# Two-block network on one core: S5 preparation in fine pieces with loads from GpSimd's queue, S5 recurrence steps behind every second weight split, first S5 outputs behind the third projection

## Chip, cores and metric

One core of a Trainium2 chip (trn2). The metric is the device time of one execution in microseconds, as the median of several runs. The kernel is one launch; weights are read from HBM once.

## The reference, cut to what matters

A sequence of 256 rows with 1024 features goes through two layers of a first block and then two layers of a second one. All is float32. A layer of the first block is

```python
h = h + 0.5 * rmsnorm(swiglu(rmsnorm(h)))       # FFN1, hidden width 2816
h = h + rmsnorm(mixer(rmsnorm(h)))
h = h + 0.5 * rmsnorm(swiglu(rmsnorm(h)))       # FFN2
```

The mixer projects its input to z, xbc, dt, u5 and two gates, and joins two branches: an SSD branch (convolution, chunked state-space sum, gated norm; four groups) and an S5 branch:

```python
step = exp(log_step); lam_bar = exp(lam * step)             # complex, 64 groups x 64 states
b_bar = ((lam_bar - 1.0) / lam)[..., None] * b
bu = einsum("blgc,gnc->blgn", u5, b_bar)
states = associative_scan(combine, (lam_bar, bu))            # s_t = lam_bar * s_(t-1) + bu_t
y = real(einsum("blgn,gcn->blgc", states, c)) + d_skip * u5
val, gate = split(gelu(y) @ w_glu)                           # then val * sigmoid(gate)
```

Everything of S5 that depends on weights alone (powers of lam_bar, products of b and c with them) is what is called S5 preparation below.

## The kernel before

**Weights and units.** Every weight matrix is streamed in units of 128x1024 floats (`unit`, L1563 and on). SyncE's queue loads a unit into a raw buffer (L1571), ScalarE casts it to a high part (`hi`, L1576), VectorE subtracts to get the low part (`lo`, L1577: this is called the split), and TensorE makes three matmuls per tile (high by high, high by low, low by high). The pair of parts comes from a ring of buffers; some entries of the ring are S5's buffers while S5 doesn't need them, and are dropped in time. During FFN1 of either layer it comes down to five pairs. `stream_b` (L1600 and on) streams column chunks: a unit is then 24 matmuls of 256 columns. `stream_k` streams a down projection: a unit is 12 matmuls of 512 columns; its last six units run the second row tile late (`TAIL`).

**FFN1 and S5 preparation.** A feed-forward stage has six chunks of hidden columns (c0 with both row tiles led by `lead_b`, c1 to c5 through `stream_b`, gate and up; 36 units in c1 to c5) and 22 units of the down projection (d0 to d21). After a chunk or unit it calls `aside`. FFN1 uses this to step a generator, `prep`, at the points of the table `PREP`: in layer 0 at c0 to c4, d0, d3, d6, d9 and d12 (constants of the mixer and S5, then four quarters q of S5, and the power tables in two halves), in layer 1 at c1, c2, c4, d1 and d6 (only the quarters). Each step is a large lump. The small matmuls of a quarter (`s5_products`, 64 of 64x64) come later, by `product()`, at points of their own. In FFN2 of layer 0 the power tables of layer 1 are made at d2 and d8.

A quarter consists of: `s5_wb` (L324 and on), which loads two tables of 512 KB from SyncE's queue (`s5B` L331 and `s5L` L333), makes four tensor operations on GpSimd (L341 to L344) and stores the result `Wd` from GpSimd's queue; `s5_cb`, two loads of 128 KB (`s5c` L351 from SyncE, `s5b` L352 from GpSimd); `s5_ct`, six VectorE products of 512 columns (L372 to L377) and two ScalarE copies; `s5_products`, the matmuls, a ScalarE copy out of PSUM, six VectorE operations (L404 to L415) and two stores `Td` from GpSimd's queue. Its big buffers are the four of the list `pp`, one each for `s5B`, `s5L`, `s5CF` and `s5bq`, so the next quarter reuses them.

**Power tables.** `s5_powers_prep(l, h)` doubles powers six times, to 63, for 16 of a layer's 32 groups of states at a time, with 36 VectorE operations (L301 to L303) per half, and stores three tables `Ed`.

**Mixer.** `mixer_body` makes u5, stores and reloads it, and puts S5's input through `s5_z`. Then the string `ORDER` says what is traced in turn: p is an SSD projection (8 units, convolution on VectorE, L569), d the time steps (1 unit), g a gate (4 units), o a quarter of the S5 outputs, c the core of an SSD group. The recurrence `s5_rec` is a generator of 14 VectorE steps for each half of the states (12 products at L545 and two scans at L549); the 28 steps are chained as `side`, and `stream_b` calls `beside()` once per unit, right behind the unit's split, which takes the next step. The outputs o0 and o1 need the first 14 steps, o2 and o3 all of them. The S5 loads of `s5_y`, the tables of the second half and SSD's broadcast rows come from GpSimd's queue.

**What sets the order.** The kernel is traced in the order of the code. A scheduler then orders each engine's instructions by readiness with the order of the code as priority; `issue_after(x)` adds the condition that the instructions traced inside it come behind x on x's own engine. With `last_lo` this holds VectorE's instructions behind the latest split, with `last_mm` TensorE's behind the latest matmul, with `last_pow` GpSimd's behind the latest norm's power. Numbered buffers (`q0` to `q16`) are shared through the lists of each stage: `X`, `W`, `A`, `E` and so on; a new use waits for the end of the old one. `X` (u5, gates, S5 loads and outputs) and `W` (two temporaries of the recurrence) share 2 and 3.

Of the kernel before, what the change touches and what calls it, by code (L numbers as in the profile page):

```python
# [30 lines left out]
ORDER = "p0 d p1 g0 g1 o0 o1 p2 c0 g2 c1 p3 o2 o3 g3 c2 c3".split()  # L31
# [4 lines left out]
    "X": [2, 3, 0, 1], "U": [4, 5], "A": [12, 13, 6, 7, 8, 9, 10, 11, 12, 13, 6, 7, 8, 9, 6, 7], "M": [15, 16],  # L36
# [42 lines left out]
class Mixer:  # L79
# [58 lines left out]
    def mix_prep(self, I):  # L138
# [109 lines left out]

        self.FL = ct.tile([P, 3, 4, NL], F32, name="FL")
        fi = t("fli")  # L250
        for d in range(4):
# [7 lines left out]
            v.tensor_scalar_mul(self.FL[:, 2, d, :], self.FL[:, 0, d, :], -1.0)  # L259

# [20 lines left out]
    def s5_powers_prep(self, l, h):  # L281


        g = self.nc.gpsimd
        tt = self.nc.vector.tensor_tensor
        Ed = self.Ed[l, h] = self.dram.tile([3, P, 1024], F32, tag="Ed", name=self.nm("Ed"), bufs=4)
        if True:
            E = [self.slot("B", "E").rearrange("p (a i) -> p a i", i=64) for _ in range(3)]
            Et = self.slot("B", "Et").rearrange("p (k a i) -> p k a i", k=2, i=32)
            x, y = Et[:, 0], Et[:, 1]  # L290
# [13 lines left out]
            for r in range(3):  # L304
                g.dma_start(Ed[r], E[r].rearrange("p a i -> p (a i)"))
# [1683 lines left out]
```

## Time and profile before

| what | us |
|---|---|
| median of 3 runs (lowest to highest) | 2936.93 (2934.03 to 2939.28) |
| the profiled execution | 2936.55 |
| its span, first to last instruction | 2934.5 |
| TensorE busy | 2814.3 (96%) |
| VectorE busy | 2181.6 (74%) |
| ScalarE busy | 1674.2 (57%) |
| GpSimd busy | 206.0 (7%) |

PE is TensorE, PEld its weight loads, DVE VectorE, ACT ScalarE, POOL GpSimd, SP SyncE. Lines (L1577) are those of the kernel before, and a helper's line stands for all its callers. A wait is the idle time of an engine before an instruction, put down to what ended it. Matmuls overlap in the pipeline, so the duration of one says little; how many start in a stretch says more. The granted clock of TensorE is a share of full speed.

### The profile page before, as it was taken

How to read it: one execution, taken by the hardware profiler on the slowest of the kernel's cores; microseconds unless marked ns; L12 is line 12 of the kernel's file. 1: busy time of each engine (PE TensorE's matmuls, PEld its weight loads, DVE VectorE, ACT ScalarE, POOL GpSimd, SP SyncE). 2: the span in 40 equal slices, each digit the busy share in tenths (PEclk: the TensorE clock that was granted, in tenths of full speed). 3: DMA queues.
4: the chain of work that ended last, by engine and by line, in shares of the span. 5: the costliest groups of instructions: out<-in, count | busy, mean ns of one | idle time of the engine just before them, and what ended most of it. 6: DMA issues, size and time to landing. Idle time of an engine off the chain costs nothing. (4 is left out here: it accounts for less than half of the span.)

```text
span 2934.5 us, 49144 instructions
## 1 busy us (share of the span) xinstructions
PE 2814.3 (96%) x19040; PEld 2508.2 (85%) x19040; DVE 2181.6 (74%) x3043; ACT 1674.2 (57%) x2389; POOL 206.0 (7%) x257
## 2 busy tenths in 40 slices
PE   8979999999999999999999999999999999999997
PEld 7968888999979888888999898987678888888886
DVE  5886877765667758777755566555589999999997
ACT  5434456545445444475554445445377777777776
POOL 2140001000004100010000000000000000000000
PEclk9999999999999999999999999999899999999998
DMA  7677565576567775656855646654589999999993
GB/s 238 199 250 242 160 204 164 197 227 188 184 223 249 241 221 174 194 155 196 264 171 180 215 154 192 186 192 132 184 279 356 343 361 361 343 359 356 354 344 145
DMA packets 350928, 687.88 MB, mean 234 GB/s; under 512 B 32672, under 2 KB 121952, under 8 KB 350688
## 3 DMA queue, kind: packets, MB, share of 16 engines
q1 hardware_dynamic: 336592, 637.42, 65.9%
q0 software_dynamic: 13952, 46.74, 4.8%
q8 instruction: 151, 2.47, 0.3%
q14 instruction: 89, 0.73, 0.1%
q10 hardware_dynamic: 144, 0.52, 0.0%
HBM read 658.05 MB, written 26.54 MB: 233 GB/s over the span
## 5 line engine op out<-in xcount | busy, mean ns | idle before, releaser
L1577 DVE TENSOR_TENSOR lo<-raw,hi 128x1024 fp32r<-128x1024 f32 x646 | 788.6, 1230 | 296.8 <-ACT hi L1576 285.1
L1576 ACT CAST hi<-raw 128x1024 fp32r<-128x1024 f32 x646 | 674.9, 1048 | 455.6 <-PE accmo L1587 84.6
L1586 PE MATMUL accmo<-lo,xg 128*128 128x512 f32 (+1 forms) x768 | 289.7, 378 | 2.3 <-DVE lo L1577 2.3
L1587 PE MATMUL accmo<-hi,xg 128*128 128x512 f32 (+1 forms) x768 | 285.2, 372 | 0.0
L1585 PE MATMUL accmo<-hi,xg 128*128 128x512 f32 (+1 forms) x768 | 274.0, 373 | 1.4 <-ACT hi L1576 1.4
L1577 DVE TENSOR_TENSOR big<-raw,big 128x1024 fp32r<-128x1024 f32 x147 | 184.9, 1259 | 110.2 <-ACT big L1576 109.3
L1576 ACT CAST big<-raw 128x1024 fp32r<-128x1024 f32 x147 | 153.7, 1049 | 168.0 <-issue 31.1
L1577 DVE TENSOR_TENSOR part<-raw,part 128x1024 fp32r<-128x1024 f32 x111 | 135.3, 1223 | 85.5 <-ACT part L1576 83.1
L1576 ACT CAST part<-raw 128x1024 fp32r<-128x1024 f32 x111 | 116.1, 1050 | 114.2 <-DMA raw<-in_ffn_w_gate_dram 17.4
L1586 PEld LDWEIGHTS accmo<-lo,xg 128*128 128x128 f32 x768 | 144.6, 188 | 32.3 <-DVE lo L1577 5.6
L1585 PEld LDWEIGHTS accmo<-hi,xg 128*128 128x128 f32 x768 | 144.6, 188 | 28.1 <-ACT hi L1576 2.6
L1587 PEld LDWEIGHTS accmo<-hi,xg 128*128 128x128 f32 x768 | 144.8, 189 | 22.5
L1586 PE MATMUL accmo<-lo,th 128*128 128x512 f32 x352 | 138.0, 392 | 0.0
L1587 PE MATMUL accmo<-hi,th 128*128 128x512 f32 x352 | 137.7, 391 | 0.0
L1577 DVE TENSOR_TENSOR lo<-big,hi 128x1024 fp32r<-128x1024 f32 x88 | 106.6, 1223 | 10.7 <-ACT hi L1576 7.6
L1585 PE MATMUL accmo<-hi,th 128*128 128x512 f32 x352 | 109.2, 391 | 0.0
L1576 ACT CAST hi<-big 128x1024 fp32r<-128x1024 f32 x88 | 92.7, 1054 | 27.0 <-PE accmo L1587 26.7
L1592 PE MATMUL accfa<-xh,lo 128*128 128x256 f32 x352 | 99.8, 284 | 0.0
L1591 PE MATMUL accfa<-xh,hi 128*128 128x256 f32 x352 | 99.7, 283 | 0.0
L1593 PE MATMUL accfa<-xl,hi 128*128 128x256 f32 x352 | 99.7, 284 | 0.0
L1577 DVE TENSOR_TENSOR lo<-more,hi 128x1024 fp32r<-128x1024 f32 x68 | 82.3, 1223 | 7.0 <-ACT hi L1576 5.0
L1576 ACT CAST hi<-more 128x1024 fp32r<-128x1024 f32 x68 | 71.4, 1053 | 19.3 <-PE accmo L1587 17.8
(993 smaller groups left out, 8603.3 us busy)
## 6 DMA issues: line engine op xcount, KB each, us to landing
raw<-in_w_gu_moe_dram SPq DMA_DIRECT2D x190, 512.0 KB, 5.3
raw<-in_w_in_dram SPq DMA_DIRECT2D x128, 512.0 KB, 4.4
raw<-in_w_down_moe_dram SPq DMA_DIRECT2D x94, 512.0 KB, 5.6
raw<-in_ffn_w_gate_dram SPq DMA_DIRECT2D x88, 512.0 KB, 4.1
raw<-in_ffn_w_up_dram SPq DMA_DIRECT2D x88, 512.0 KB, 4.3
raw<-in_ffn_w_down_dram SPq DMA_DIRECT2D x88, 512.0 KB, 4.2
big<-in_w_gu_moe_dram SPq DMA_DIRECT2D x60, 512.0 KB, 5.7
more<-in_w_gu_moe_dram SPq DMA_DIRECT2D x46, 512.0 KB, 5.7
```

What stands on the lines that cost most here:

```text
L1576: nc.scalar.copy(hi, raw)
L1577: self.last_lo = nc.vector.tensor_tensor(lo, raw, hi.bitcast(F32), op=ALU.subtract).ins
L1585: mm(ps, lh, rh, start=first, stop=False)
L1586: mm(ps, lh, rl, start=False, stop=False)
L1587: self.last_mm = mm(ps, ll, rh, start=False, stop=last).ins
L1591: mm(ps, lh, rh, start=first, stop=False)
L1592: mm(ps, ll, rh, start=False, stop=False)
L1593: self.last_mm = mm(ps, lh, rl, start=False, stop=last).ins
```

## The change

- `ORDER`: p2 now comes before o0 and o1. The list `X` is longer, so that 2 and 3 stay free for the recurrence until the second gate g2.
- `beside()` takes a step only every `pace`-th unit. `pace` is 2 inside the projections p0, p1 and p3, and 1 otherwise.
- The table `PREP`, `product()` and the list of late products go. `prep` becomes `side` at the end of chunk 0 (layer 0) or 1 (layer 1) of FFN1, with one step behind every unit's split; `stream_k` calls `beside()` too, for the units ahead of its tail. What is left behind FFN1 is run off there.
- The generators yield much more often: 17 pieces of the constants, 11 of the powers, five for each quarter (two coefficient products in each of the first three, nothing in the fourth, the small matmuls and what follows them in the fifth).
- `s5B`, `s5L` and `s5c` are loaded from GpSimd's queue instead of SyncE's.
- `s5_powers_prep(l)` makes powers to 31 for all 32 groups at once (30 VectorE operations), in six doublings less one, and ScalarE copies them out to tables of 64, the lower half conjugated and in reverse. Layer 0's come before the quarters, layer 1's from the end of chunk 4 of FFN2.
- In the products, the first masked copy moves from VectorE to ScalarE.

The diff, cut to its core (the added bare `yield` lines of `mix_prep` are left out):

```diff
-ORDER = "p0 d p1 g0 g1 o0 o1 p2 c0 g2 c1 p3 o2 o3 g3 c2 c3".split()
+ORDER = "p0 d p1 g0 g1 p2 o0 o1 c0 g2 c1 p3 o2 o3 g3 c2 c3".split()
...
-    "X": [2, 3, 0, 1], "U": ...
+    "X": [2, 3, 0, 1, 0, 1, 0, 1, 0] + [2, 3, 1, 0] * 5, "U": ...
...
-PREP = (
-    ("c0 c1 c2 c3 c4 d0 d3 d6 d9 d12".split(), "d0 d4 d10 d15".split()),
-    ("c1 c2 c4 d1 d6".split(), "c4 d1 d6 d11".split()),
-)
...
-    def s5_powers_prep(self, l, h):
+    def s5_powers_prep(self, l):
+        E = [self.slot("B", "E").rearrange("p (a i) -> p a i", i=32) for _ in range(2)]
+        Et = self.slot("B", "Et").rearrange("p (k a i) -> p k a i", k=2, i=16)
+        x, y = Et[:, 0], Et[:, 1]
+        for r in range(2):
+            g.memset(E[r][:, :, 0], 1.0 - r)
+            cp(E[r][:, :, 1], self.s4dir[:, r, l * 32 : l * 32 + 32])
+        for n in (1, 2, 4, 8, 16):
+            k = min(n, 31 - n)
+            b = [e[:, :, n : n + 1].to_broadcast([P, 32, k]) for e in E]
+            for r, op in ((0, ALU.subtract), (1, ALU.add)):
+                tt(x[:, :, :k], E[0][:, :, 1 : k + 1], b[r], op=ALU.mult)
+                if n > 8:
+                    yield
+                tt(y[:, :, :k], E[1][:, :, 1 : k + 1], b[1 - r], op=ALU.mult)
+                tt(E[r][:, :, n + 1 : n + 1 + k], x[:, :, :k], y[:, :, :k], op=op)
+                if n > 4:
+                    yield
+            if n < 8:
+                yield
+        for h in range(2):
...
+            for r in range(2):
+                g.memset(F[r][:, :, 0], 0.0)
+                cp(F[r][:, :, 32:], E[r][:, hs])
+                self.nc.scalar.activation(F[r][:, :, 1:32], E[r][:, hs, :0:-1], AF.Copy, scale=1.0 - 2.0 * r)
+            g.memset(F[2][:, :, 0], 0.0)
+            cp(F[2][:, :, 1:], self.s4len[:, ls].unsqueeze(2).to_broadcast([P, 16, 63]))
             for r in range(3):
-                g.dma_start(Ed[r], E[r].rearrange("p a i -> p (a i)"))
+                g.dma_start(Ed[r], F[r].rearrange("p a i -> p (a i)"))
+            yield
...
         cb = [self.s5_cb(I, l, 0)]
-        yield
+        if l == 0:
+            yield from self.s5_powers_prep(0)
         for q in range(4):
             self.s5_wb(I, l, q)
             if q < 3:
                 cb.append(self.s5_cb(I, l, q + 1))
-            self.late.append(self.s5_ct(l, q, *cb.pop(0)))
-            yield
-            if l == 0 and q in (1, 2):
-                self.s5_powers_prep(0, q - 1)
-                yield
+            yield from self.s5_ct(l, q, *cb.pop(0))
...
-        nc.sync.dma_start(B, I["s5_bT"][l, q])
+        nc.gpsimd.dma_start(B, I["s5_bT"][l, q])
...
-        nc.sync.dma_start(Lb, ld.unsqueeze(1).to_broadcast([8, 16, 1024]))
+        nc.gpsimd.dma_start(Lb, ld.unsqueeze(1).to_broadcast([8, 16, 1024]))
...
-        self.nc.sync.dma_start(cc, I["s5_cT"][l, q])
+        self.nc.gpsimd.dma_start(cc, I["s5_cT"][l, q])
...
         tt(u, ce(1), fl(1), op=ALU.mult)
+        yield
         tt(Cv[:, :, 0], Cv[:, :, 0], u, op=ALU.add)
         tt(Cv[:, :, 1], ce(0), fl(1), op=ALU.mult)
+        yield
...
-        return lambda: self.s5_products(q, p0, bq, CF, s)
+        yield
+        yield
+        with self.tc.issue_after(self.last_mm):
+            self.s5_products(q, p0, bq, CF, s)
+        yield
...
-        nc.vector.tensor_scalar_mul(T, K, self.jm[:, 0:1])
+        nc.scalar.activation(T, K, AF.Copy, scale=self.jm[:, 0:1])
...
     def beside(self):
+        self.beat += 1
+        if self.beat % self.pace:
+            return
         with self.tc.issue_after(self.last_lo):
             next(self.side, None)
...
         def proj(g):
+            self.pace = 1 if g == 2 else 2
             pr[g] = self.ssd_proj(W, l, g, xh, xl)
+            self.pace = 1
...
             if i < nk - kk * tail:
+                self.beside()
+            if i < nk - kk * tail:
                 go(0, u, k0)
                 go(1, u, k0)
-                if aside:
-                    aside(f"d{i}")
...
             if w == f"c{l}":
                 self.ring_drop((6, 7), (8, 9))
-            if w in at[1]:
-                self.product()
-            if w in at[0]:
-                with self.tc.issue_after(self.last_lo), self.tc.issue_after(self.last_pow.ins):
-                    next(steps, None)
+                self.side = self.prep(I, l)
+                if l == 0:
+                    with self.tc.issue_after(self.last_lo), self.tc.issue_after(self.last_pow.ins):
+                        next(self.side)
-        return self.swiglu(*xT, *w, aside)()
+        banks = self.swiglu(*xT, *w, aside)()
+        with self.tc.issue_after(self.last_lo):
+            for _ in self.side:
+                pass
+        return banks
...
-            if l == 0 and w in ("d2", "d8"):
-                with self.tc.issue_after(self.last_lo):
-                    self.s5_powers_prep(1, "d2 d8".split().index(w))
+            if l == 0 and w == "c4":
+                self.side = self.s5_powers_prep(1)
```

## Rows read from the trace of the kernel before

**Rows 1.** The page: busy time by engine; the costliest group of ScalarE.
```profile
PE 2814.3 (96%) x19040; PEld 2508.2 (85%) x19040; DVE 2181.6 (74%) x3043; ACT 1674.2 (57%) x2389; POOL 206.0 (7%) x257
...
L1576 ACT CAST hi<-raw 128x1024 fp32r<-128x1024 f32 x646 | 674.9, 1048 | 455.6 <-PE accmo L1587 84.6
```
**Rows 2.** Stretches: us, then busy us (instructions) of PE, PEld, DVE, ACT, POOL, clock.
```profile
50.00:100.00 50.00, 50.00 (x419) 50.00 (x418) 35.08 (x90) 25.02 (x36) 0.00 (x0) 1.00 0.62 181
311.50:400.70 89.20, 77.72 (x582) 75.90 (x577) 81.85 (x110) 37.16 (x61) 3.25 (x6) 0.90 0.53 166
400.70:432.50 31.80, 31.32 (x402) 30.34 (x402) 19.60 (x31) 17.20 (x30) 2.67 (x5) 1.00 0.67 215
...
856.30:1051.00 194.70, 193.12 (x1478) 177.43 (x1478) 133.28 (x153) 90.46 (x120) 50.57 (x38) 0.99 0.74 234
```
**Rows 3.** TensorE's instructions by tile: ns min/median/max, first to last start; layers 0, 1.
```profile
L1585 PE MATMUL accfa<-hi,hh x52: 387/389/628, 150.3 to 238.5; 128*128 128x512 f32 x52
...
L1585 PE MATMUL accfa<-big,hh x36: 387/389/628, 152.4 to 239.9; 128*128 128x512 f32 x36
...
L1585 PE MATMUL accfa<-big,hh x40: 389/389/504, 988.2 to 1055.7; 128*128 128x512 f32 x40
...
L1585 PE MATMUL accmx<-part,xh x16: 389/389/792, 247.7 to 268.3; 128*128 128x512 f32 x16
...
L1585 PE MATMUL accmx<-part,xh x16: 387/389/498, 1059.8 to 1079.3; 128*128 128x512 f32 x16
```
**Rows 4.** Timeline near 195 us: start, us, instructions merged.
```profile
194.81 0.81 PE L396 MATMUL zfa<-s5CF,s5bq 64*64 64x64 f32 x20
```
**Rows 5.** TensorE's waits from 100 to 262 us: total, times, longest.
```profile
PE zfa L396 <- DVE s5CF L374: 7.5, 1, 7.5
...
PE accfa L1591 <- DVE ht L1827: 2.8, 1, 2.8
```
**Rows 6.** SyncE's waits from 100 to 262 us: total, times, longest.
```profile
SPq L333 <- POOL s5B L342: 19.9, 3, 9.2
...
SPq L331 <- DMA Wd<-s5B: 18.5, 3, 11.1
```
**Rows 7.** GpSimd's operations on s5t from 100 to 262 us: ns min/median/max.
```profile
L341 POOL TENSOR_TENSOR s5t<-s5B,s5L x4: 2413/2862/4560, 127.0 to 207.3; 128x1024 f32<-128x1024 f32 x4
L343 POOL TENSOR_TENSOR s5B<-s5B,s5t x4: 1264/1468/2150, 132.3 to 216.0; 128x512 f32<-128x512 f32 x4
```
**Rows 8.** VectorE's S5 operations by tile from 100 to 262 us: ns min/median/max.
```profile
L375 DVE TENSOR_TENSOR s5CF<-s5c,FL x4: 684/685/2905, 127.0 to 205.4; 128x512 f32<-128x512 f32 x4
...
L301 DVE TENSOR_TENSOR Et<-E,E x12: 199/352/2422, 157.6 to 233.0; 128x16 f32<-128x16 f32 x2, 128x32 f32<-128x32 f32 x2, 128x64 f32<-128x64 f32 x2, 128x128 f32<-128x128 f32 x2
L302 DVE TENSOR_TENSOR Et<-E,E x12: 190/248/669, 157.7 to 233.5; 128x16 f32<-128x16 f32 x2, 128x32 f32<-128x32 f32 x2, 128x64 f32<-128x64 f32 x2, 128x128 f32<-128x128 f32 x2
...
L414 DVE SCALAR_TENSOR_TENSOR s5u<-s5u,jm x12: 343/480/2498, 167.1 to 241.4; 128x384 f32<-128x384 f32 x4, 128x256 f32<-128x256 f32 x4, 128x128 f32<-128x128 f32 x4
```
**Rows 9.** DMA issues from 100 to 262 us: KB each, median us to landing.
```profile
Wd<-s5B POOLq DMA_DIRECT2D x4, 512.0 KB, 7.5
...
s5c<-in_s_cT_dram SPq DMA_DIRECT2D x4, 128.0 KB, 6.4
...
s5b<-in_s_bS_dram POOLq DMA_DIRECT2D x2, 128.0 KB, 6.8
```
**Rows 10.** GpSimd's issue of the s5b load by tile: ns min/median/max.
```profile
L352 POOL DMA_DIRECT2D s5b<-in_s_bS_dram x6: 541/551/601, 174.1 to 999.7; - x6
```
**Rows 11.** The recurrence of layer 0 on VectorE by tile: ns min/median/max.
```profile
L545 DVE TENSOR_TENSOR S<-S x4: 1205/1212/1219, 317.7 to 397.2; 128x1024 f32<-128x1024 f32 x4
...
L549 DVE TENSOR_TENSOR_SCAN S<-s5E,S x4: 2272/2283/2285, 322.2 to 384.8; 128x1024 f32<-128x1024 f32 x4
```
**Rows 12.** VectorE's groups from 311.5 to 400.7 us: busy us, mean ns, idle before.
```profile
L1577 DVE TENSOR_TENSOR part<-raw,part 128x1024 fp32r<-128x1024 f32 x6 | 7.3, 1214 | 0.5 <-ACT part L1576 0.5
...
L569 DVE SCALAR_TENSOR_TENSOR cv<-accpa,cw,cv 128x255 f32<-128x255 f32 (+2 forms) x12 | 5.1, 471 | 0.0
```

More of the change, by code (lines that the diff above doesn't have):

```diff
@@ L264, in mix_prep @@
         cmul(*u2, (cs, sn), (cs, sn))
+        yield
         cmul(self.s4dir[:, 0], self.s4dir[:, 1], u2, u2)
@@ L279, in mix_prep @@
         dma(self.lsd.rearrange("k a x -> a k x"), lt.rearrange("p g j r n -> p (g j) (r n)"))
-    def s5_powers_prep(self, l, h):
+    def s5_powers_prep(self, l):
         g = self.nc.gpsimd
+        cp = self.nc.scalar.copy
         tt = self.nc.vector.tensor_tensor
[L286 to L290, printed above, removed]
-            ls = slice(l * 32 + h * 16, l * 32 + h * 16 + 16)
-            g.memset(E[2][:, :, 0], 0.0)
-            self.nc.scalar.copy(E[2][:, :, 1:], self.s4len[:, ls].unsqueeze(2).to_broadcast([P, 16, 63]))
-            for r in range(2):
-                g.memset(E[r][:, :, 0], 1.0 - r)
-                self.nc.scalar.copy(E[r][:, :, 1], self.s4dir[:, r, ls])
-            for n in (1, 2, 4, 8, 16, 32):
-                k = min(n, 63 - n)
-                b = [e[:, :, n : n + 1].to_broadcast([P, 16, k]) for e in E[:2]]
-                for r, op in ((0, ALU.subtract), (1, ALU.add)):
-                    tt(x[:, :, :k], E[0][:, :, 1 : k + 1], b[r], op=ALU.mult)
-                    tt(y[:, :, :k], E[1][:, :, 1 : k + 1], b[1 - r], op=ALU.mult)
-                    tt(E[r][:, :, n + 1 : n + 1 + k], x[:, :, :k], y[:, :, :k], op=op)
@@ new lines, in s5_powers_prep @@
+        E = [self.slot("B", "E").rearrange("p (a i) -> p a i", i=32) for _ in range(2)]
[10 more added lines that the diff above has]
+                if n > 8:
+                    yield
+                tt(y[:, :, :k], E[1][:, :, 1 : k + 1], b[1 - r], op=ALU.mult)
+                tt(E[r][:, :, n + 1 : n + 1 + k], x[:, :, :k], y[:, :, :k], op=op)
+                if n > 4:
+                    yield
+            if n < 8:
+                yield
@@ new lines, in s5_powers_prep @@
+        for h in range(2):
+            Ed = self.Ed[l, h] = self.dram.tile([3, P, 1024], F32, tag="Ed", name=self.nm("Ed"), bufs=4)
+            hs = slice(h * 16, h * 16 + 16)
+            F = [self.slot("B", "Eh").rearrange("p (a i) -> p a i", i=64) for _ in range(3)]
+            for r in range(2):
[3 more added lines that the diff above has]
+            g.memset(F[2][:, :, 0], 0.0)
+            ls = slice(l * 32 + h * 16, l * 32 + h * 16 + 16)
+            cp(F[2][:, :, 1:], self.s4len[:, ls].unsqueeze(2).to_broadcast([P, 16, 63]))
@@ L373, in s5_ct @@
         tt(u, ce(1), fl(1), op=ALU.mult)
+        yield
         tt(Cv[:, :, 0], Cv[:, :, 0], u, op=ALU.add)
         tt(Cv[:, :, 1], ce(0), fl(1), op=ALU.mult)
+        yield
         tt(u, ce(1), fl(2), op=ALU.mult)
@@ L383, in s5_ct @@
             )
-        return lambda: self.s5_products(q, p0, bq, CF, s)
+        yield
+        yield
+        with self.tc.issue_after(self.last_mm):
+            self.s5_products(q, p0, bq, CF, s)
+        yield
     def s5_products(self, q, p0, bq, CF, s):
@@ L1431, in __init__ @@
         self.side = iter(())
+        self.beat, self.pace = 0, 1
         self.Ed = {}
@@ L1842, in ffn1 @@
         w = [I[f"ffn1_w_{k}"][l] for k in ("gate", "up", "down")]
-        steps = self.prep(I, l)
-        at = PREP[l]
         def aside(w):
@@ L1887, in prep @@
         yield from self.s5_prep(I, l)
-    def product(self):
-        with self.tc.issue_after(self.last_mm):
-            self.late.pop(0)()
     def first_body(self, I, h):
```

4 lines of the change are left out of this document (3 added, 1 removed).

## Prediction

> **What bounds the kernel now.** I read the page first, then busy time by stretches, then where TensorE's instructions of a stage start and end, then who waited for whom. TensorE is busy for 2814.3 us, 96% of the span [rows 1], so only its idle and slowed time can be won, and only where the change works: the first feed-forward stage (FFN1) of layers 0 and 1, the two mixers, and FFN2 of layer 0.
>
> An undisturbed stretch sets the pace: 419 matmuls of 256 columns in 50 us [rows 2], 0.119 us each. One weight unit of a column stage has 24 of them, so TensorE needs a split unit every 2.86 us.
>
> FFN1 of the two layers does the same TensorE work, so layer 1 is the yardstick for layer 0. The down projection runs from 150.3 to 239.9 in layer 0, 89.6 us, and from 988.2 to 1055.7 in layer 1, 67.5 us [rows 3]: 22.1 more. Layer 0 has four product runs of S5 in that stretch and layer 1 three; a run is 64 small matmuls, 20 of which took 0.81 us [rows 4], so 2.6 us, and 19.5 us stay as loss. The step to the mixer's first matmul takes 7.8 us (239.9 to 247.7) against 4.1 [rows 3], 3.7 more. Before the down projection TensorE waited once for 2.8 us [rows 5]. Layer 0's FFN1 thus loses **26.0 us**, its longest wait 7.5 us for VectorE's S5 coefficients [rows 5]. Layer 1 loses little: busy 193.1 of 194.7 us [rows 2].
>
> Why there? SyncE carries all weights in order, and S5's loads stand in the same line: it stood 19.9 us on three s5L loads, for GpSimd to free the buffer, and 18.5 us on three s5B loads [rows 6], with weights behind them. And GpSimd's tensor operations (2.4 to 4.6 us each, [rows 7]) hold VectorE up: a short product lasted up to 2.42 us against 0.20 at best, one of 512 columns 2.91 against 0.68 [rows 8].
>
> In the mixer, from the first projection to the second gate (p0, d, p1, g0, g1), VectorE is the bound: busy 81.9 of 89.2 us, while TensorE did 582 matmuls at a mean granted clock of 0.90 [rows 2], that is, after its waits it ran in part at the lower of its two levels, 1.2 instead of 2.4 GHz. At 0.119 that work is 69 us: **20 us** lost per layer. The next 31.8 us (o0, o1, p2) have VectorE at 19.6 [rows 2].
>
> **The change, part by part.** *FFN1, layer 0.* The prep becomes 48 small pieces, one behind each unit's split from the second column chunk on; the five parts of the ring and the order in the code put the last at the eleventh of the down projection's 22 units. SyncE loses 12 loads per layer, and with them the 38 us of rows 6. VectorE's powers fall from 72 products to 30: 12 of each of six sizes at 0.19 to 0.67 us [rows 8], 24 us, become 6 of each of five sizes, about 10.7. The mirrored upper half is made by ScalarE, ten copies per layer, none longer than a weight's cast of 1.05 us [rows 1], so up to 10 us, covered by its idle half (90.5 of 194.7 busy, [rows 2]); without that cover the weights' hi casts, and so VectorE's splits, would be late by as much.
>
> What remains is dense in the last 20 pieces, the four quarters of S5. Per quarter TensorE needs 5 x 2.86 + 2.6 = 16.9 us, 67.6 for four. VectorE needs 20 splits of 1.22 [rows 12], 24.4; 4 to 9, I take 6.6, for the FFN's own products (estimated from layer 1's 133.3 us busy, [rows 2], less 66 splits and the quarters, with and without 15 us of blocking); per quarter six coefficient products of 0.685 and five shorter operations of 0.34 to 0.48 [rows 8], about 6.1, so 24.4; in all 55 us, plus blocking by GpSimd. That is bounded below by nothing and above by GpSimd's shortest operations, 2 x 2.41 + 2 x 1.26 = 7.3 per quarter [rows 7], 29: between 55 and 85 us against 67.6. VectorE can start four units ahead (five parts), 11.4 us, so 0 to 6 us remain as waits. I take 5, nearer the upper end, since rows 8 show blocking whenever GpSimd works. Gain 26 - 5 = **21 us**; ends 12 (GpSimd's operations coincide badly) and 26.
>
> Products can't wait for their coefficients as at 219 us: these are finished two pieces earlier, ahead of a split that TensorE needs first. The mask's first product moves from VectorE to ScalarE, eight of under 0.7 us; the three behind it now wait for ScalarE's queue, with the next split behind them: in the 5 us.
>
> *FFN1, layer 1.* The quarters move from the third column chunk to the fifth instead of being spread to the down projection. The same 55 to 85 against 67.6, less 11.4 of lead: 0 to 6, and GpSimd's queue may add; it lost 1.6 before. I take **2 us lost**, ends 0 and 8.
>
> *FFN2, layer 0.* Two lumps of powers become eleven pieces, half the work. Layer 1's FFN1 shows such work hidden under TensorE; 0, ends -1 and +2.
>
> *GpSimd's queue.* It takes 24 loads, issued at about 0.55 us each [rows 10], 13 us on an engine busy for 206 us in all [rows 1]. Sizes alike land alike: 128 KB in 6.8 us from GpSimd's queue, 6.4 from SyncE's [rows 9]. What they wait for is now waited for here: the buffer that the previous quarter's store must leave (7.5 us to land, [rows 9]). Behind stand the quarter's other stores, gains and the powers of the norms; the pieces end half a down projection before the norm, which hides it.
>
> The Trainium skill (SBUF — State Buffer, section "SBUF: two separate sides") warns that a DMA from GpSimd's queue cannot get its descriptors written while VectorE holds the port they share, and advises SyncE or ScalarE: 0.62 us alone became 3.1. By that rule a quarter's three loads would cost 7.4 us more; by the pair in rows 9 it is 0.4 us a load.
>
> *Mixers.* VectorE's 28 steps of the S5 recurrence (24 of 1.21, 4 scans of 2.28, [rows 11]) went one behind each unit. Units count 8 for p0, 1 for d, 8 for p1, 4 each for g0 and g1. Before, 25 steps lay behind them; now 4 + 1 + 4 + 4 + 4 = 17. Steps 18 to 25 (six products, two scans: 11.8 us) go to p2, the last three to g2. So the bound stretch shortens by 11.8 us of its 20 lost. p2 gives some back: 8 splits (9.8), 12 convolution steps of 0.47 (5.6, [rows 12]) and 11.8 make 27.2 us against 22.9 of TensorE, 4.3 lost; and o0, o1, now behind p2, no longer lengthen its cover. That leaves 7.5. After it VectorE has no lead, has the o's products and the c0 core due, and 3.6 us in g2 that were not there; the nearest row, 19.6 busy of 31.8, has room, but behind. I charge 1.5: **6 us per layer, 12 in all**; ends 0 and 18. The first outputs' four table loads, in GpSimd's queue, move behind p2 with them; their buffers are free since the gates' stores, so they land early. The second half's table loads wait in GpSimd's queue for the first half's end, in g1, and have two units, 5.7 us, to land.
>
> **Sum**: -21 + 2 + 0 - 12 = -31 us, against the profiled execution's 2936.55 (span 2934.5 and 2 around it), 0.4 below the median: 2905.5, say 2906.
>
> **Rivals.** (1) *The lock keeps FFN1's gain.* The hold behind a split names VectorE alone; GpSimd runs its operations as soon as loads land, in bursts. For it: rows 8; against: layer 1 took 50 us of GpSimd with 1.6 us lost. Layer 0 gains 10, layer 1 loses 7, mixers 12: -15, 2922. This is also how the fine pieces would not be fine.
> (2) *GpSimd's queue becomes the bound; slower.* The next quarter's coefficients overwrite a buffer that is stored from GpSimd's queue. If that store stands behind the next load's wait, VectorE waits, and with it every split. A chain of store landing 7.5, load landing 7.5, four operations 8.5 (medians about 2.86, 2.86, 1.47, 1.30) and six issues of 0.55 is 26.8 us per quarter against 16.9: 4 x 9.9 less 11.4 is 28 us in each layer. Layer 0 +2, layer 1 +27, mixers -12: +17, 2954. It decides from 24.6 us per quarter on, where 2 x (4 x 7.7 - 11.4) = 39 eats both gains and layer 1's 1.6. Against: two pieces without coefficients lie in between, and loads can run ahead. With the skill's figure the chain would be 34 us; nothing in rows 9 supports that.
> (3) *The mixers give nothing*, since p2, c0 and g2 stall for what g1 no longer does: 2906 + 12 = 2918.
> (4) *All hidden*: 26 in layer 0, 18 in the mixers, none lost: -44, 2892.
>
> **The numbers.** Forecast 0.48, (1) 0.17, (2) 0.12, (3) 0.13, (4) 0.10. The range reaches from (4) past (1), down to little gain in FFN1: 2890 to 2931, which leaves out (2) and the edges. A measurement can tell 0.2% (5.9 us) from no change. Faster by more: 0.85; within 0.05; slower 0.10.
>
> **What would show it.** Right: no SyncE wait on S5 loads; layer 0's down projection near 72 us; the wait for the coefficients gone; the mixer from p0 to the last of p2 and o1 some 114 instead of 121 us, with VectorE's steps running past g1. Wrong: VectorE idle on a store from GpSimd's queue (2); stretched VectorE products beside GpSimd's and waits for splits in layer 1's column chunks (1); waits for splits in p2 and g2 of over 8 us (3).

## The result, and the profile after

The changed kernel takes 2967.5 us (median of 4, 2964.31 to 2971.61) against 2935.48 for the kernel before on the same chip: ratio 1.0116, 95% interval [1.0102, 1.013]. It is 1.2% slower; 2906 was forecast, and the range ended at 2931. The profiled execution's span is 2962.5 us, 28.0 more than before's. Line numbers from here on are the changed kernel's; from `s5_wb` on they are 17 to 30 above those of before.

The page's busy time by engine, as [rows 1]:

```profile
PE 2818.3 (95%) x19040; PEld 2512.3 (85%) x19040; DVE 2173.9 (73%) x2951; ACT 1686.3 (57%) x2409; POOL 213.6 (7%) x285
```

VectorE works 8 us less and GpSimd 8 more, TensorE's share hardly moves: the 28 us are waits and slowed stretches. TensorE's instructions by tile, as [rows 3] (the first three rows are from 100 to 400 us, the others from 870 us on):

```profile
L1615 PE MATMUL accfa<-hi,hh x52: 388/389/497, 157.9 to 234.2; 128*128 128x512 f32 x52
L1615 PE MATMUL accfa<-big,hh x36: 388/389/628, 159.9 to 235.6; 128*128 128x512 f32 x36
L1615 PE MATMUL accmx<-part,xh x16: 387/389/792, 249.1 to 270.3; 128*128 128x512 f32 x16
...
L1615 PE MATMUL accfa<-big,hh x40: 389/389/396, 1017.1 to 1076.2; 128*128 128x512 f32 x40
L1615 PE MATMUL accmx<-part,xh x16: 389/389/498, 1080.4 to 1099.9; 128*128 128x512 f32 x16
```

Layer 0's down projection runs from 157.9 to 235.6, 77.7 us instead of 89.6, but the step to the mixer takes 13.5 instead of 7.8, and the mixer's first matmul is 1.4 us later than before. In layer 1 it is 20.6 us later. A ledger by the start of the same instruction in both traces, where the last column is what each stage adds:

| from, to | before | after | adds |
|---|---|---|---|
| first transpose | 10.14 | 22.98 | +12.8 |
| first matmul of FFN1's second chunk | 40.3 | 49.8 | -3.3 |
| mixer's first matmul, layer 0 | 247.7 | 249.1 | -8.1 |
| first matmul of the gated outputs (accgl), layer 0 | 500.1 | 512.4 | +10.9 |
| first matmul of FFN2, layer 0 | 663.8 | 672.9 | -3.2 |
| FFN1's first, layer 1 | 855.3 | 864.2 | -0.2 |
| mixer's first, layer 1 | 1059.8 | 1080.4 | +11.7 |
| accgl, layer 1 | 1312.1 | 1338.5 | +5.8 |
| FFN2's first, layer 1 | 1475.1 | 1501.1 | -0.4 |
| end of the span | 2934.5 | 2962.5 | +2.0 |

The first accgl matmul is no clean end of a mixer: the last cores still run beside the gated outputs, and some of what is lost ahead of it is won back behind it. FFN2's first matmul is the firmer mark. By it the mixers lost 7.8 and 5.4 us.

**The start.** Timeline of GpSimd, of VectorE and of TensorE in the changed kernel:

```profile
9.54 0.48 POOL L194 DMA_DIRECT2D sd<-in_s_d_dram  x1 [3.73 <-DMA gn<-in_ffn_pre_g_dram]
10.01 0.58 POOL L368 DMA_DIRECT2D s5c<-in_s_cT_dram  x1
...
13.40 1.44 POOL L1778 TENSOR_TENSOR sm<-sm,mhalf 128x1 f32<-128x1 f32 x1
...
21.04 1.23 DVE L1607 TENSOR_TENSOR lo<-raw,hi 128x1024 fp32r<-128x1024 f32 x1 [5.22 <-ACT hi L1606]
22.18 1.41 DVE L1801 SCALAR_TENSOR_TENSOR xn<-h,sm,gn 128x512 f32<-128x512 f32 x2
...
22.98 1.97 PE L1760 MATMUL tr<-ident,xn 128*128 128x128 f32 x8 [22.98 <-DVE xn L1801]
```

and in the kernel before:

```profile
7.48 0.56 POOL L1748 TENSOR_TENSOR sm<-sm,mhalf 128x1 f32<-128x1 f32 x1 [3.44 <-DVE sm L1747]
...
9.34 1.42 DVE L1771 SCALAR_TENSOR_TENSOR xn<-h,sm,gn 128x512 f32<-128x512 f32 x2 [1.94 <-DMA gn<-in_ffn_pre_g_dram]
```

S5's loads now stand ahead of the first norm's power on GpSimd (7.48 became 13.40), and the scheduler put five splits ahead of the norm's product on VectorE; the last of them waits 5.22 us for the cast of its weights. The late power is 5.9 of the 12.8 us at the first transpose; the rest is lost behind it, since the power is done at 14.84 and the product starts at 22.18.

**FFN1.** Waits of TensorE from 100 to 262 us, of VectorE from 948 to 972, of TensorE from 864 to 1083:

```profile
PE trfa L1760 <- DVE xn L1801: 10.8, 1, 10.8
PE zfa L419 <- DVE s5CF L392: 6.8, 1, 6.8
...
DVE s5CF L389 <- DMA Td<-s5CF: 5.2, 1, 5.2
...
PE accfa L1621 <- DVE ht L1857: 11.0, 1, 11.0
```

and GpSimd's timeline in layer 1, with one line of VectorE's:

```profile
950.53 0.66 POOL L350 DMA_DIRECT2D s5L<-lsd  x1
951.19 0.55 POOL L363 DMA_DIRECT2D Wd<-s5B  x1
951.72 0.55 POOL L369 DMA_DIRECT2D s5b<-in_s_bS_dram  x1
961.94 0.54 POOL L348 DMA_DIRECT2D s5B<-in_s_bT_dram  x1 [9.67 <-DMA Wd<-s5B]
962.46 0.54 POOL L442 DMA_DIRECT2D Td<-s5CF  x1
969.27 2.33 POOL L358 TENSOR_TENSOR s5t<-s5B,s5L 128x1024 f32<-128x1024 f32 x1 [6.27 <-DMA s5B<-in_s_bT_dram]
...
970.56 1.59 DVE L389 TENSOR_TENSOR s5CF<-s5c,FL 128x512 f32<-128x512 f32 x1 [5.18 <-DMA Td<-s5CF]
```

In layer 1 this is rival (2) to the letter. GpSimd stands 9.67 us at the next load, because its buffer is still being stored to Wd; the coefficients' store Td stands behind that issue; VectorE stands for Td until 970.56, and with it everything behind, the FFN's product `ht` among it, for which TensorE waits 11.0 us. GpSimd's quarters follow each other there at 24.8, 24.8 and 29.2 us (starts of the first operation on s5t). VectorE was crowded already. The window from 908.9 to 948.9 us, with the columns of [rows 2]:

```profile
908.90:948.90 40.00, 40.00 (x425) 39.52 (x425) 37.06 (x39) 20.38 (x27) 20.81 (x18) 1.00 0.79 264
```

and one of VectorE's groups in it:

```profile
L427 DVE TENSOR_TENSOR dd<-delta,sd 128x128 f32<-128x128 f32 x2 | 3.0, 1478 | 0.0
```

37.06 of 40 us busy. Of the two products of 128 columns in that group one took 0.29 us; the other, which began at 918.72 with an operation of GpSimd's beginning at 918.82, took 2.67.

In layer 0 the longest wait is the one for the mixer's first norm (`xn`), 10.8 us against 5.2 before. GpSimd's last quarter, and VectorE's splits beside it:

```profile
224.42 2.37 POOL L358 TENSOR_TENSOR s5t<-s5B,s5L 128x1024 f32<-128x1024 f32 x1 [3.88 <-DMA s5B<-in_s_bT_dram]
226.87 2.38 POOL L359 TENSOR_TENSOR s5B<-s5B,s5L 128x1024 f32<-128x1024 f32 x1
...
227.43 6.55 DVE L1607 TENSOR_TENSOR part<-raw,part 128x1024 fp32r<-128x1024 f32 x2 [4.28 <-ACT part L1606]
```

Two splits that take 1.22 us each elsewhere last 6.55, just ahead of the norm.

**Mixer.** Windows of layer 0 after the change: p0 to g1; p2; g2 with o0 and o1; from c0's first transposes to the last gate, g3. The second fence has the kernel before: p0 to g1, and from c0 to g3.

```profile
305.90:392.30 86.40, 80.87 (x701) 79.25 (x698) 77.31 (x113) 39.45 (x65) 3.26 (x6) 0.94 0.59 182
392.30:422.20 29.90, 26.27 (x194) 25.73 (x193) 24.31 (x28) 13.42 (x22) 0.00 (x0) 0.89 0.52 159
422.20:450.00 27.80, 27.80 (x374) 26.80 (x375) 15.33 (x19) 13.48 (x22) 2.65 (x5) 1.00 0.71 224
450.00:497.30 47.30, 36.29 (x401) 31.55 (x400) 36.74 (x75) 27.19 (x61) 6.59 (x10) 0.89 0.40 120
```

```profile
304.20:400.70 96.50, 84.36 (x700) 82.05 (x697) 89.15 (x122) 39.90 (x65) 3.25 (x6) 0.91 0.55 169
...
432.50:485.20 52.70, 51.38 (x564) 48.30 (x564) 41.35 (x77) 34.30 (x71) 7.50 (x10) 1.00 0.59 177
```

The first half is 10.1 us shorter, as forecast. The loss is behind it. Before, o0 and o1 were done inside p2's stretch, c0 began at 432.4, and TensorE had 564 matmuls to do in the 52.7 us to g3. Now c0 begins at 449.9 with 401 left, g2 and part of p3 already spent, and TensorE is busy for 36.3 of 47.3 us. Its waits from 449 to 500 us are, but for the gate's (accgd), for the cores' own chain:

```profile
PE trca L752 <- DVE dg L751: 2.5, 2, 2.3
PE trca L722 <- DVE M L717: 2.4, 1, 2.4
PE trcb L722 <- DVE M L717: 2.2, 1, 2.2
PE accgd L1621 <- ACT zs L669: 2.1, 1, 2.1
PE trca L742 <- POOL zs L740: 1.7, 1, 1.7
```

The kernel before had 2.3 us of waits from 432 to 500. The mean granted clock is 0.89 instead of 1.00: behind its waits TensorE runs in part at the lower of its two levels, 1.2 instead of 2.4 GHz.

### The profile page after: what moved, and what is told of

The parts are those of the page before. It is cut to its first block, busy times and chain, and to the rows that moved or that the text cites. A ratio compares the mean times of both kernels' runs of the same rounds, so it can differ in the third digit from the quotient of the medians.

```text
span 2962.5 us, 49062 instructions
## 1 busy us (share of the span) xinstructions
PE 2818.3 (95%) x19040; PEld 2512.3 (85%) x19040; DVE 2173.9 (73%) x2951; ACT 1686.3 (57%) x2409; POOL 213.6 (7%) x285
## 5 line engine op out<-in xcount | busy, mean ns | idle before, releaser
L1607 DVE TENSOR_TENSOR lo<-raw,hi 128x1024 fp32r<-128x1024 f32 x646 | 799.3, 1246 | 298.3 <-ACT hi L1606 289.5
L1617 PEld LDWEIGHTS accmo<-hi,xg 128*128 128x128 f32 x768 | 145.1, 189 | 22.5
L1778 POOL TENSOR_TENSOR sm<-sm,mhalf 128x1 f32<-128x1 f32 x32 | 21.5, 673 | 919.4 <-DVE sm L1777 919.3
```

Source lines behind the costliest of these rows:

```text
L1607: self.last_lo = nc.vector.tensor_tensor(lo, raw, hi.bitcast(F32), op=ALU.subtract).ins
L1617: self.last_mm = mm(ps, ll, rh, start=False, stop=last).ins
L1778: self.last_pow = nc.gpsimd.tensor_tensor(r, v, self.mhalf, op=ALU.pow)
```

## The experiments

Profiled executions differ where nothing was changed. With the same instructions, FFN1 of layer 1 took 211.9 to 221.0 us in the kernels below, FFN1 of layer 0 223.8 to 231.1, and all from layer 1's FFN2 on, some 1460 us, 1458.1 to 1463.7. Medians carry the verdicts; the stages say where. The kernels were timed on several chips, on which the kernel before took 2932.2 to 2936.7, so kernels of different chips are compared by their ratios to before (0.1% is 2.9 us). FFN1 is from its first matmul to the mixer's first, the mixer from there to the first accgl; the column "both, to FFN2" has the two mixers together, to FFN2's first matmul instead.

| kernel | first transpose | FFN1, 0 | mixer, 0 | FFN1, 1 | mixer, 1 | both, to FFN2 | median | ratio to before |
|---|---|---|---|---|---|---|---|---|
| before | 10.1 | 235.8 | 252.4 | 204.5 | 252.3 | 831.3 | 2932.2 to 2936.7 | 1 |
| after | 23.0 | 224.3 | 263.3 | 216.2 | 258.1 | 844.5 | 2967.5 | 1.0116 [1.0102, 1.013] |
| e1_mixer_back | 22.9 | 231.1 | 252.2 | 211.9 | 253.9 | 835.6 | 2954.2 | 1.0065 [1.0048, 1.0082] |
| e2_order_back | 22.9 | 229.5 | 256.4 | 218.8 | 254.6 | 837.1 | 2961.5 | 1.0096 [1.0079, 1.0112] |
| e3_pace_one | 22.1 | 225.8 | 257.8 | 221.0 | 265.8 | 850.9 | 2975.9 | 1.0124 [1.0098, 1.015] |
| e4_hold_start | 9.4 | 226.1 | 265.5 | 216.9 | 264.1 | 851.1 | 2963.6 | 1.0112 [1.0095, 1.0129] |
| e5_cf_store | 22.7 | 224.9 | 263.5 | 214.4 | 260.0 | 845.1 | 2958.6 | 1.0082 [1.0059, 1.0104] |
| e6_sync_loads | 16.7 | 222.7 | 263.3 | 214.4 | 257.2 | 845.5 | 2954.5 | 1.0064 [1.0041, 1.0087] |
| e7_mixer_alone | 9.6 | 236.0 | 260.3 | 203.3 | 263.8 | 844.5 | 2949.3 | 1.0059 [1.0039, 1.0078] |
| g1_wide_l1 | 22.5 | 223.8 | 261.2 | 212.4 | 260.9 | 842.6 | 2960.1 | 1.0085 [1.0066, 1.0103] |
| g2_two_b | 9.9 | 217.7 | 261.8 | 208.8 | 261.4 | 847.7 | 2948.9 | 1.0047 [1.0028, 1.0065] |
| h1_best_old_mixer | 9.5 | 217.8 | 252.0 | 206.4 | 257.3 | 831.2 | 2923.8 | 0.997 [0.9956, 0.9984] |
| h2_core_first | 10.0 | 223.1 | 257.9 | 206.9 | 254.4 | 838.8 | 2925.6 | 0.9982 [0.9969, 0.9995] |
| h3_cf_store | 10.0 | 223.1 | 251.1 | 208.1 | 254.6 | 827.4 | 2925.8 | 0.9974 [0.9962, 0.9985] |
| i1_no_hold | 22.7 | 215.7 | 251.6 | 208.2 | 259.1 | 826.5 | 2929.2 | 0.9992 [0.9982, 1.0003] |
| i2_one_buffer | 9.9 | 229.9 | 251.2 | 213.7 | 249.4 | 827.1 | 2934.5 | 0.9998 [0.9988, 1.0009] |
| i3_no_wide | 9.9 | 221.8 | 249.8 | 208.8 | 255.4 | 826.6 | 2923.6 | 0.9966 [0.9953, 0.9979] |

### The mixer's edits

e1: the changed kernel, all three undone; e2: its first line alone; e3: its last line alone; e7: the reverse of e1, on the kernel before.

```diff
-ORDER = "p0 d p1 g0 g1 p2 o0 o1 c0 g2 c1 p3 o2 o3 g3 c2 c3".split()
+ORDER = "p0 d p1 g0 g1 o0 o1 p2 c0 g2 c1 p3 o2 o3 g3 c2 c3".split()
-    "X": [2, 3, 0, 1, 0, 1, 0, 1, 0] + [2, 3, 1, 0] * 5, "U": ...
+    "X": [2, 3, 0, 1], "U": ...
-            self.pace = 1 if g == 2 else 2
+            self.pace = 1
```

> The changed kernel with the mixer's three edits undone (ORDER, X and the step behind every unit as before); FFN1's and FFN2's S5 preparation stays changed. Theory: from the end of FFN1's norm to the gated outputs the mixer lost 8.0 us in layer 0 and 5.4 in layer 1, and that is the mixer edits' own doing; so 2967.5 - 13.4 = 2954 us (2949 to 2959), still slower than the kernel before, with the late first transpose (near 23 us) and the wait of some 11 us in layer 1's FFN1 both still there. Rival: the mixers are late because of what FFN1 leaves behind in GpSimd's queue (stores, loads traced early); then the edits are worth nothing and it stays at 2965 to 2969.

> The changed kernel with only the string ORDER as before (p2 behind o0 and o1 again); the step behind every second unit and the list X stay. Theory: what the mixers lost lies in their second half (12 us in layer 0, 11.4 in layer 1), where the chain of the core c0 and c1 (ScalarE's exponentials, VectorE's masks) lost p2's eight units as its cover, while the first half gained 4.3 and 6.0 by the slower recurrence; so both second halves come back and the gains stay: 2967.5 - 23 = 2944 us (2939 to 2952). Rival: it is the recurrence that ends later, with the second half's table and output loads waiting for it in GpSimd's queue; then the order alone gives little: 2962 to 2968, and waits around c0 and c1 stay.

> The changed kernel with a recurrence step behind every unit again (pace 1); the new ORDER stays. With pace and ORDER both undone it took 2954.2 us and the mixers (their first matmul to the gated outputs) 252.2 and 253.8 us; with ORDER alone undone 256.4 and 254.6; as changed 263.3 and 258.1. Theory: ORDER costs by itself some 7 and 3.5 us, whatever the pace, since the S5 outputs o0 and o1 now stand between p2 and the core c0 and push c0 some 17 us later: mixers near 259 and 257, the whole 2954 + 10 = 2964 us (2960 to 2968). Rival: ORDER only hurts together with the pace, since then the recurrence's last steps and the loads behind them come late in p2 and g2; then mixers near 252 and 254 and 2951 to 2957 us.

> The kernel before with the mixer's three edits alone (ORDER, X, pace); FFN1 and FFN2 as before. Theory: these edits lose time by themselves, some 11 us in layer 0 and 6 in layer 1 (mixers 263 and 258 us instead of 252.4 and 252.3), with nothing of FFN1's change in the way: 2936 + 17 = 2953 us (2947 to 2959). Rival: part of the mixers' loss comes from S5's loads and stores that FFN1's change put into GpSimd's queue; then the mixers take 252 to 256 us and the whole 2936 to 2944 us.

e1 came out at 2954.2, its mixers at 252.2 and 253.9 us: the theory's number. (Its profiled span is only 7.1 us shorter, since FFN1 of layer 0, which it doesn't touch, took 6.8 more.) e7 is the mirror: 2949.3, slower than before with FFN1 untouched, so the rival of a leftover in GpSimd's queue falls. e2 missed: 2961.5 instead of 2944. The old order brings back only 6.9 and 3.5 us of the mixers. The theory had added the first half's gain to a second half as before; without the new order the slower recurrence loses that gain again, around p2 and p3. TensorE's waits in p2 and p3 of layer 0 (380 to 515 us), the four longest, are

```profile
PE accpd L1622 <- DVE lo L1607: 3.0, 1, 3.0
PE trcb L722 <- DVE M L717: 2.6, 2, 1.7
PE accpc L1621 <- DVE cv L596: 2.5, 1, 2.5
PE zoa L518 <- DMA s5CF<-Td: 2.0, 1, 2.0
```

e3 shows the order's price without the pace: 257.8 and 265.8. Both mixers together, to FFN2's first matmul: 826.5 to 835.6 us in the seven kernels with neither edit, 842.6 to 851.1 in the seven with both, 850.9 with the order and not the pace (e3), 837.1 with the pace and not the order (e2). Against the means of the two groups (829 and 846) the order costs some 9 us together with the pace and 21 without it; the pace costs 8 or nothing, which lies within the spread of 9. The longer list X is in both e2 and e3 and was not tried alone; e2, 1.5 us from e1, gives no sign that it costs anything. e3's total ran past its range, by a second mixer of 265.8 where 257 was expected and by the 221.0 us of an FFN1 that it doesn't touch.

### The start

e4: every piece of layer 0's FFN1, not the first alone, is held behind the first power.

```diff
-                if l == 0:
-                    with self.tc.issue_after(self.last_lo), self.tc.issue_after(self.last_pow.ins):
-                        next(self.side)
+                if l == 0:
+                    self.front = self.last_pow.ins
+                    self.beside()
...
+            if self.front is not None:
+                c.enter_context(self.tc.issue_after(self.front))
```

> The changed kernel with every piece of layer 0's FFN1 preparation held behind the first norm's power on GpSimd (not its first piece alone). Theory: the first transpose starts at 22.98 us instead of 10.14 because GpSimd issues S5's small loads ahead of that power; held behind it, the start is back near 10 us and the whole gains 12.8: 2955 us (2951 to 2959). Rival: the time at the start is used (units are split ahead, so FFN1's first chunk then runs faster), and the shift is given back by waits in chunk 0 and 1: 2961 to 2968, with the first transpose near 10 us all the same.

The first transpose is back at 9.36, but the ratio to before fell only from 1.0116 to 1.0112, some 1 us instead of 12.8 (the bare medians, of two chips, differ by 3.9), and the two intervals overlap. In the trace FFN1's second chunk starts at 38.9 instead of 49.8, so 10.9 remain behind the first chunk (with weights split ahead it goes faster: 2.7 are won back), and 9.4 at layer 1's FFN1. The mixers, whose code is that of the changed kernel, took 6.6 us longer to FFN2 in this execution, the top of the range that such mixers show (842.6 to 851.1). So e4 shows where the late start comes from, and not what it is worth; i1, further on, weighs it again.

### GpSimd's queue and the density

e5 moves one store, e6 three loads, g1 spreads layer 1's pieces, g2 (on e4) gives s5B a second buffer.

```diff
e5
-        nc.gpsimd.dma_start(d[:, :1024], CF)
+        nc.scalar.dma_start(d[:, :1024], CF)
e6
-        nc.gpsimd.dma_start(B, I["s5_bT"][l, q])
+        nc.sync.dma_start(B, I["s5_bT"][l, q])
...
g1
                 self.side = self.prep(I, l)
+                self.pace = 1 + l
g2
-        B, Lb = (self.slot("pp", n) for n in ("s5B", "s5L"))
+        B, Lb = self.slot("pB", "s5B"), self.slot("pp", "s5L")
```

In g2, `pB` is [6, 5] and `pp` [7, 8, 9]; e6 treats s5L and s5c like s5B.

> The changed kernel with one of the two stores of a quarter (the coefficients s5CF, 512 KB) issued from ScalarE's queue instead of GpSimd's. Theory: in layer 1 TensorE waits 11.0 us because VectorE waits for that store, which stands in GpSimd's queue behind the issue of the next quarter's load, which itself waits 9.7 us for the store Wd; and the 6.8 us wait for the coefficients in layer 0 has the same cause. With the store elsewhere layer 1's FFN1 loses its 11.6 and layer 0 some 3 to 7 of its wait: 2967.5 - 16 = 2951 us (2947 to 2957). Rival: the cycle of load, four operations and Wd's store on GpSimd, some 25 us per quarter, is the bound whatever the other store does; then another wait takes its place: 2961 to 2968.

> The changed kernel with S5's three loads (s5B, s5L, s5c) issued by SyncE again; the fine pieces stay. Theory (GpSimd's queue is what costs FFN1): the store of the coefficients no longer stands behind a load's wait on GpSimd, so layer 1's 11.0 us wait shrinks to 3 or less, and the start comes back in part, since fewer issues stand ahead of the first power; SyncE's weights stand a few us behind the buffers again. FFN1 of layer 1 from 216 to some 208 to 212 us, first transpose at 14 to 20 us, the whole 2950 to 2961 us. Rival: the density of the pieces is what costs; moving loads back only adds SyncE's waits (38.4 us of them in the kernel before), and it takes 2968 to 2985 us.

> The changed kernel with layer 1's FFN1 pieces behind every second unit (20 pieces over 40 units, to the down projection) instead of behind every unit; all else stays. Theory: a quarter then has 10 units, some 28 us of TensorE, more than the 24.6 to 25.5 us that load, four operations and store take on GpSimd, and VectorE (92% busy from 908.9 to 948.9 us) has room: the 11.0 us wait goes, FFN1 of layer 1 takes 205 to 208 us instead of 216, the whole 2957 us (2954 to 2962). Rival: the queue's order alone (the store behind the load's wait) sets the wait, wherever the pieces lie: the wait moves into the down projection and the whole stays at 2964 to 2970 us.

> The kernel with all pieces held behind the first power (2963.6 us), and a second buffer for s5B, so that the next quarter's load does not wait for the store Wd of the one before. Theory: GpSimd's cycle of 25 us per quarter is mostly load (6 to 7 us), operations (9) and store (7 to 9) in a row; with two buffers the load overlaps, the coefficients' store is no longer behind a wait, and the waits of 4.7 (layer 0) and 10.2 us (layer 1) go: 2963.6 - 13 = 2951 us (2946 to 2957). Rival: GpSimd's operations then come denser and hold VectorE up more in the same place; the waits go only in part: 2958 to 2966 us.

e5: VectorE waits for no store in layer 1 any more, TensorE's wait of 11.0 us is two of 3.5 in all, and the median falls by 8.9; but the two intervals of the ratios just touch, so the gain is not clear of noise. The stage is only 1.8 us shorter: GpSimd still loads, works and stores in a row, every 24.4 to 25.5 us. So the store was the longest wait, not the bound.

e6: 2954.5, 13 us less. The start is back in part (16.66), and VectorE waits for no Td in layer 1. SyncE stands for S5's buffers again (20.2 us at s5B, 26.7 at s5L in layer 1). The rival's 2968 and more is far off, so SyncE's waits cost no more than GpSimd's did; but layer 1's FFN1 took 214.4, not the theory's 208 to 212, and TensorE's longest wait there fell to 5.9 and not to 3. The median is in the range; the stage is not what put it there.

g1: 2960.1, inside the theory's range, and the longest wait falls to 4.4; but 212.4 us for the stage lies within the spread of unchanged kernels, so the stage itself proves nothing.

g2: layer 0's FFN1 at 217.7, layer 1's at 208.8, below all kernels with the fine pieces and one buffer; the ratio falls from e4's 1.0112 to 1.0047, some 19 us (14.7 between the medians of the two chips). GpSimd's timeline in layer 1:

```profile
890.37 0.59 POOL L348 DMA_DIRECT2D s5B<-in_s_bT_dram  x1
890.98 2.42 POOL L359 TENSOR_TENSOR s5B<-s5B,s5L 128x1024 f32<-128x1024 f32 x1
...
905.85 2.52 POOL L358 TENSOR_TENSOR s5t<-s5B,s5L 128x1024 f32<-128x1024 f32 x1 [5.88 <-DMA s5L<-lsd]
...
925.00 3.05 POOL L358 TENSOR_TENSOR s5t<-s5B,s5L 128x1024 f32<-128x1024 f32 x1 [1.34 <-DMA s5L<-lsd]
```

The load no longer waits for a store, and a quarter takes 18.4 to 19.2 us (887.46, 905.85, 925.00). The rival of denser operations falls by the total, and layer 1's wait went from 10.2 to 3.7 us; but in layer 0 the waits for the coefficients did not go (5.4 in all, 4.7 in e4). What went there is the wait for the mixer's first norm, from 12.7 to 4.4: GpSimd's last quarter begins at 188.4 and no longer runs beside the last splits. This divides all kernels: that wait is 9.5 to 17.8 us in the nine with fine pieces and one buffer, 2.4 to 6.2 in the six with two.

### Put together, and taken apart again

h1: the hold, two buffers, layer 1 at every second unit, and the mixer of before. h2: the same FFN1 with the changed mixer, but c0 between o0 and o1. h3: h1 with e5's store. i1, i2, i3: h1 without the hold, without the second buffer, without the spacing.

```diff
h2
-ORDER = "p0 d p1 g0 g1 p2 o0 o1 c0 g2 c1 p3 o2 o3 g3 c2 c3".split()
+ORDER = "p0 d p1 g0 g1 p2 o0 c0 o1 g2 c1 p3 o2 o3 g3 c2 c3".split()
```

> The changed kernel with all pieces held behind the first power, two buffers for s5B, layer 1's pieces behind every second unit, and the mixer of before. Theory: the three causes are separate and add: start as before; FFN1 of layer 0 at 218 us instead of 235.8, of layer 1 at 205 to 206 instead of 204.5; mixers at 252 to 254 each as before. That is 2936 - 18 + 1 + 1 = 2920 us (2915 to 2926), faster than both kernels. Rival: the gains overlap or FFN1's gain returns in the mixer, as the start's did in part: 2928 to 2937 us.

> The same FFN1 (held pieces, two buffers, layer 1 behind every second unit) with the changed mixer, but the core c0 between the outputs o0 and o1 instead of behind both. Theory: the mixers lose because o0 and o1 stand between p2 and c0; with one of them behind c0 half of what ORDER costs (5 and 3 us) comes back: mixers from 262 to 257 us each, second halves from 115 to 118 down to 111; the whole 2949 - 3 - 10 = 2936 us (2931 to 2942). Rival: c0 waits for S5's loads in GpSimd's queue or VectorE's recurrence steps, wherever it stands: mixers stay at 260 to 263, the whole 2943 to 2950 us.

> As the kernel with the mixer of before (held pieces, two buffers, layer 1 behind every second unit), and the coefficients' store from ScalarE's queue. Theory: with two buffers that store no longer stands behind a load's wait, so moving it gives nothing more: within 4 us of that kernel, 2916 to 2924 us. Rival: layer 0's waits for coefficients (5.4 us in all with two buffers) still come from this store; then 3 to 5 us less: 2914 to 2917 us. If ScalarE's casts are held up by it, up to 5 us more.

> The fastest kernel so far (2923.8 us; held pieces, two buffers, layer 1 behind every second unit, mixer of before) without the hold behind the first power. Theory: the start is late again (first transpose near 22 us instead of 9.5) and nothing after it makes up for it: 2923.8 + 12.8 = 2936.6 us (2932 to 2941), no better than the kernel before. Rival: what is late at the start is won back later, as the small effect of the hold alone seemed to say: 2922 to 2929 us, with the first transpose near 22 us all the same.

> The same fastest kernel with one buffer for s5B. Theory: GpSimd's cycle of load, operations and store in a row is back: FFN1 of layer 0 from 218 (223 in two like it) to 224 to 230 us, of layer 1 from 206 to 209 to 213; together 8 to 14 us: 2935 us (2931 to 2940). Rival: with layer 1 spread out and the pieces held, the loads have time to wait: 2923 to 2928 us.

> The same fastest kernel with layer 1's pieces behind every unit. Theory: with two buffers GpSimd's cycle is short enough, the spacing is worth little: FFN1 of layer 1 at 208 to 210 us instead of 206.4, the whole 2926 us (2922 to 2930). Rival: VectorE's 92% in the dense stretch is what costs layer 1: 214 to 219 us there, 2932 to 2938 us.

h1 beats both kernels: 0.997 [0.9956, 0.9984], 9 us less than before. It misses 2920 by 4, inside the range. Its first matmul in the mixer comes at 229.1 us, 18.6 earlier than before. h2: with c0 only one place earlier the mixers are at 257.9 and 254.4 instead of 261.8 and 261.4 in g2; its total is even 10 us below what was expected, and on the same chip only 1.8 above h1's, with intervals that overlap. That is the second witness that o0 and o1 ahead of c0 are the loss. h3 gives nothing on top, as the theory said (2925.8, 1.8 past its range).

i3 equals h1: with two buffers the spacing is worth nothing, so i3, timed on the chip of i1 and i2, is the mark for both. i1 is 5.6 us above it, between the theory's 12.8 and the rival's nothing, and the intervals are apart; its second chunk starts 9.8 us later than h1's (49.0 against 39.2). i2 is 10.9 above it: the second buffer is worth as much as expected.

## Why the prediction was wrong, step by step

- **The start was not in the sum.** It counted GpSimd's issues at 0.55 us each and asked only which norm stands behind the pieces at FFN1's end. The first norm stands on the same engine, and the diff narrows the hold (`last_pow`) from every piece to the first. Missing: 12.8 us at the first transpose, 9.5 behind the first chunk; worth 5.6 us between i3 and i1, and some 1 us, less than the noise, between the changed kernel and e4.
- **FFN1 of layer 0, -21: it was -8** (from the second chunk on). "Products can't wait for their coefficients" failed: 6.8 us, because VectorE's coefficients themselves waited 8.8 us for the store that they overwrite. "The pieces end half a down projection before the norm" failed too: GpSimd's fourth quarter begins at 224.4 and runs to 233, since the quarters follow each other at 27.6 us (141.7 to 224.4 for three), not at 16.9; it stretches the splits ahead of the norm, and the step to the mixer takes 13.5 us. With that cycle shortened the stage of 235.8 us is 13 to 18 shorter (223.1 to 217.7 in g2, h1, h2 and i3, which share it), against 21 forecast: most of the gain was there, and the queue took it.
- **FFN1 of layer 1, +2: it was +11.7**, by the mechanism of rival (2), whose point of decision was a cycle of 24.6 us (24.8 to 29.2 here); its own price for this layer, 27, was too high. Its total, 2954, was no hit either: it left out the start and took the mixers at -12. "Loads can run ahead" was the step that failed: the load needs the buffer that Wd is being stored from. The s5c loads of 128 KB landed in 3.7 and 4.9 us (medians of layers 0 and 1) from GpSimd's queue, against 6.4 and 5.3 from SyncE's before. What cost was the order of the queue. The warning of the Trainium skill (SBUF — State Buffer, "SBUF: two separate sides"), whose 0.62 and 3.1 us are for a DMA beside a copy on VectorE, doesn't show in these medians; VectorE's work here is mostly splits and products of two inputs.
- **FFN2, 0: right**, -0.2 us from its first matmul to the next FFN1's.
- **Mixers, -12: it was +13** to FFN2's first matmul, +16.7 to the first accgl. The shortened first half was right (10.1 us in layer 0, 11.8 forecast). The step that failed is that o0 and o1 "no longer lengthen" p2's cover: it looked only at what p2 gains or loses, not at what stands behind o0 and o1 in TensorE's order. That is c0, and for c0 and c1 the units of g2 and p3 are the cover. From p0's first matmul to the last of p2 and o1 it took 139.5 us (305.9 to 445.4) instead of 128.3 (304.2 to 432.5), where 7 less were forecast.
- **Right:** SyncE's waits for S5 loads are gone (GpSimd waits in its place); the recurrence runs past g1; the named sign of rival (2), VectorE idle on a store from GpSimd's queue, is what the profile shows in layer 1. Beside it stands rival (1)'s sign, VectorE's operations stretched beside GpSimd's (2.67 us for 0.29; 6.55 for two splits).

Not settled: where the remainder of the start's 9.5 us goes in the medians. With the mixer of before, kernels with two buffers take 104 to 107 us from p2 to accgl in layer 1, those with one 99; this is no loss, for to FFN2's first matmul their second mixers take 413.3 to 416.5 us, those with one buffer 414.0 to 417.7.

## What to carry to other kernels

When loads move to another engine's queue, write down that queue's whole order from the first instruction of the kernel on, and look for any store whose issue stands behind a load's wait; give that load a second buffer before moving the store. When a piece of work is moved in TensorE's order, ask what then starts later behind it and which work was that one's cover. A hold that is narrowed from all pieces to the first one lets the scheduler move the others to the kernel's start.

## What was not expected of the hardware

Loads from GpSimd's queue were as fast as from SyncE's: s5B of 512 KB landed in 7.0 us from the one and 7.7 from the other (medians of four in layer 1). But what stood in GpSimd's queue in both kernels landed later there: s5b in 6.7 us instead of 4.4, Wd in 8.0 instead of 5.8. And code that no edit touches differed by up to 9 us between profiled executions where it is full of waits (FFN1 of layer 1), and by 5.6 us in the 1460 us at the end; single stages of single profiles settle nothing below that.
